# Two expert streams emitted in turn, row tile by row tile, with side work as jobs that hold a PSUM bank

## The chip, the core and the metric

The kernel runs on one core of a Trainium2 chip. The core has five engines that run their own instruction streams in order: TensorE (PE; its weight loads are shown apart as PEld), VectorE (DVE), ScalarE (ACT), GpSimd (POOL) and SyncE (SP, which issues most transfers). They wait for each other by semaphores. Data lies in SBUF; matmuls write to PSUM, which has eight banks of 128 partitions x 512 fp32 numbers. The metric is the device time of one execution in microseconds (us), lower is better. Times are medians of several executions, and one execution is recorded by the profiler.

## The reference

The program is two transformer blocks over 512 tokens of width 1024, all in fp32: a first block with a retention and pooling mixer, a mixture of experts and a gated projection, and a second block of attention. The change lies in the mixture of experts and in the step behind it:

```python
logits = xt @ router_w + router_b
top_vals, top_idx = lax.top_k(logits, 4)          # 4 of 32 experts for each token
gates = softmax(top_vals)
order = argsort(top_idx.reshape(-1)); tok = order // 4; xs = xt[tok]
gu = lax.ragged_dot(xs, w_gu, group_sizes) + b_gu[sorted_e]     # 1024 -> 2048
gate = minimum(gu[:, ::2], 7.0); up = clip(gu[:, 1::2], -7.0, 7.0)
act = (up + 1.0) * (gate * sigmoid(1.702 * gate))
y = lax.ragged_dot(act, w_down, group_sizes) + b_down[sorted_e] # 1024 -> 1024
out = zeros_like(xt).at[tok].add(y * gates[order][:, None])
...
h = h + out
gate = sigmoid(rms_norm(h, norm_ple_w) @ ple_gate_w); h = h + gate * (p @ ple_proj_w)
```

Each expert has 1024 x 2048 and 1024 x 1024 fp32 weights, 12 MB, which are read once.

## The kernel before

A fp32 product is made of three (or four) products of a shorter format: each operand is cut into a high part (a rounding copy) and a low part (the number minus its high part). For weights this is done on the chip. A row tile is 128 rows x 1024 columns of a weight matrix; ScalarE makes its high part `wh` (L877) and VectorE its low part `wl` (L878). An expert has 24 row tiles in three runs of 8: gate_up half 0, gate_up half 1, down. The function `chunks` (L864) walks over a run.

The experts are sorted by their count of tokens at run time, and the program alternates between a place for many and a place for few tokens (`LESS[e]`). A *few* expert has up to 64 tokens: high and low part of its x lie side by side as 128 columns, and a row tile takes 4 matmuls of 512 columns (L882). The two halves of the result are then added by the *fold*: ScalarE copies the accumulator to SBUF (`gs`, L939), and 8 matmuls with a constant put it, transposed and added, into a transposition bank (`tr`, L938). A *many* expert has up to 96 tokens: 6 matmuls of 512 columns a row tile (`mm3`, L165 to L167). The activation follows each gate_up run: two clamps on VectorE (`ag`, L910, and `au`, L911), read from the fold's bank or, for many, straight from the accumulator; a gelu on ScalarE (L912); a product on VectorE (L913); for many four transposes; then the split of the result `a` into its high part (ScalarE, L216) and low part (VectorE, L217). The same pair of lines splits the turned input `x`. After a down run the accumulator is scaled on ScalarE (`ys`, L948), and GpSimd adds its rows to the DRAM buffer `y_d` by an indirect transfer (L950). Rows of x come by an indirect gather (`xg`, L837), from tables (`slots`, L718 and on) that are made for batches of 2, 2, 4, 8, 8 and 8 experts.

The order of the work: expert e's runs come as gate_up half 0 of e, down of e-1, gate_up half 1 of e. As few and many experts alternate, so do their runs, by 8 row tiles. Side work (turning x, clamps, fold, scatter, tables) is a list of steps each due a fixed number of row tiles after it was put there (`later`, `next_tile`, L811 on). A scheduler in the framework then orders the instructions of each engine, so the program's order and the written one differ in places.

Buffers: weights arrive in 1 MB loads of two row tiles, issued by SyncE (`load`, L145) into seven buffers; the split pairs `wh`, `wl` are six. PSUM has three accumulators of two banks (`mm`) and two banks for transposes (`tr`). The gated bias of the down projection (`gated_bias`, L1026) is one product of the gates with the bias matrix; it uses four accumulators in turn (L1051) and is copied to `h` (L1052). The stage `back` loads `y_d` (L1154), adds it to `h` (L1159), multiplies by the norm's gain `g_ple` (L1160) and goes on to the next norm.

Of the kernel before, what the change touches and what calls it, by code (L numbers as in the profile page):

```python
# [18 lines left out]
S = 512  # L19
D = 1024  # L20
# [12 lines left out]
BATCHES = {0: 2, 2: 2, 4: 4, 8: 8, 16: 8, 24: 8}  # L33
# [16 lines left out]
def const_tables():  # L50
# [11 lines left out]
    t["sel"] = ((p[:, None] % 32 == np.arange(32)[None, :]) & (p[:, None] < 64)).astype(f32)  # L62
# [55 lines left out]
    return {"c_small": small, "c_lasting": lasting, "c_decay": decay, "c_band": band, "c_rope2": rope2}, cols  # L118


class Kern:
# [92 lines left out]
    def split_in(self, ps, dst, sl):  # L214
        dh, dl = dst
        self.nc.scalar.activation(dh[:, :, sl], ps, AF.Copy)  # L216
        self.nc.vector.tensor_tensor(out=dl[:, :, sl], in0=ps, in1=dh[:, :, sl].bitcast(F32), op=ALU.subtract)  # L217
# [91 lines left out]
    def run(self):  # L309
        tc, nc, I = self.tc, self.nc, self.I  # L310
        with ExitStack() as g:
# [8 lines left out]
            with ExitStack() as a:  # L320
# [382 lines left out]
    def slots_by(self, i0, n, T, ps, late=None):  # L703
# [23 lines left out]
        gi = T.tile([128, n], I32, tag=pre + "gi", name="gi")  # L727
        gt = T.tile([128, n], F32, tag=pre + "gt", name="gt")
# [8 lines left out]
    def arrange(self, P, T, sel):  # L737
# [14 lines left out]
        nc.vector.tensor_scalar(sel, c["ranks"][:, 0:NE], rank[:, 1:2], None, op0=ALU.is_equal)  # L752
# [30 lines left out]
    def moe(self, f, Q):  # L783
        tc, nc, I, c = self.tc, self.nc, self.I, self.c
        self.psum(f, "m", 3, 2)
# [3 lines left out]
        sel = P.tile([128, NE], F32R, name="sel")  # L789
# [3 lines left out]
        bt = P.tile([128, 2 * D], F32R, name="bt")  # L793
        nc.gpsimd.memset(bt.bitcast(F32)[64:128, :], 0.0)
        ys = P.tile([128, 2, D], F32, name="ys")
        braw = ys.rearrange("p a n -> p (a n)")
        for r in (0, 32):
            nc.scalar.dma_start(braw[r:r + 32, :], I["expert_b_gate_up"][0])
# [9 lines left out]
        self.at_tile, self.late = 0, []  # L808

        def later(stages):  # L810

            self.late += [(self.at_tile + d, fn) for d, fn in stages]

        def now(stages):
            for _, fn in stages:
                fn()

        def next_tile(n=1):
            self.at_tile += n
            while due := [a for a in self.late if a[0] <= self.at_tile]:  # L820
                a = min(due, key=lambda a: a[0])
                self.late.remove(a)
                a[1]()
# [5 lines left out]
        def table(e):  # L829

            ps = self.mm.tile([128, 2, 512], F32, tag="mm", name="mm")
            gen = self.slots_by(e, BATCHES[e], Q, ps[:, 0, :])
            later([(j, lambda: next(gen)) for j in range(BATCHES[e])] + [(BATCHES[e] + 2, lambda: tables(e, next(gen)))])

        def gather(e):
            m = FEW if LESS[e] else CAP
            nc.gpsimd.indirect_dma_start(out=xgs[e % 2][0:m], out_offset=None, in_=self.hn_d[:, :],  # L837
# [3 lines left out]
        def pair(m, tag):  # L841

            t = T.tile([128, 8, 2 * m], F32R, tag=tag, name=tag)
            return t[:, :, 0:m], t[:, :, m:2 * m], t

        def turned(x, m):

            p = pair(m, "x2")
            tp = {}

            def begin(j):
                tp[j] = self.transpose4(x, 4 * j, m=m)

            def end(j):
                self.split_in(tp[j], [a[:, 4 * j:4 * j + 4] for a in p[0:2]], slice(0, m))
            return p, [(1, lambda: begin(0)), (3, lambda: begin(1)), (4, lambda: end(0)), (6, lambda: end(1))]

        def turn(e):
# [714 lines left out]
```

## Time and profile before

| quantity | value |
|---|---|
| median of 3 runs | 1866.92 us (1865.54 to 1868.93) |
| profiled execution | 1864.25 us |
| its span | 1862.5 us, mean granted clock 0.979 |
| TensorE busy | 1762.6 us, 95% |
| VectorE busy | 1535.5 us, 82% |
| ScalarE busy | 1186.7 us, 64% |
| GpSimd busy | 188.2 us, 10% |
| DMA | 491.10 MB, mean 264 GB/s |
| first and last row tile of an expert | about 236.5 and 1392.6 us |

The experts take 1156 us of the 1862.5, from the first `wl` of L878 to the last. The rest lies before (the mixer) and after (the gated projection and the second block) and is left as it is, but for the first steps behind the experts. A share of busy time here is an average over stages with unlike limits, so the rows further down are cut from stretches inside the experts. A stretch of 48 row tiles is one many and one few expert. Matmuls are pipelined, so the spans of neighbouring matmuls overlap: the time from start to start is what one costs.

### The profile page before, as it was taken

The page shows a single profiled execution, that of the slowest core. Times are in us where ns is not written, and L with a number is a line of the kernel's source. Part 1 is how long each engine was busy: PE and PEld are TensorE (multiplying, and loading weights), DVE is VectorE, ACT ScalarE, POOL GpSimd, SP SyncE. Part 2 cuts the span into 40 slices and gives each one's busy share as a digit, 9 for nine tenths or more (in the row PEclk, how much of TensorE's full clock was granted, in tenths as well). Part 3 has the DMA queues.
Part 4 walks back from the last instruction along what each step waited for, and adds up shares of the span by engine and source line. Part 5 has one row for each costly group of instructions (what it writes and reads, how often), then busy time and mean ns, then how long its engine had stood idle before and what let it go on. Part 6 is the DMA issues. An engine that isn't in the chain of part 4 may idle for free.

```text
span 1862.5 us, 24800 instructions
## 1 busy us (share of the span) xinstructions
PE 1762.6 (95%) x8378; PEld 1278.2 (69%) x8379; DVE 1535.5 (82%) x2637; ACT 1186.7 (64%) x1584; POOL 188.2 (10%) x120
## 2 busy tenths in 40 slices
PE   8999779899999899999999999999998999999999
PEld 6887547666666566666666666666666877787776
DVE  5574479799999789999999999999987869999542
ACT  5224258677778777777877777877875545564431
POOL 0011210121111011311110210210100000000000
PEclk9999879999999899999999999999998999999999
DMA  8225568999999999999999999999986222211211
GB/s 282 89 85 170 164 208 314 335 367 373 361 381 375 337 340 380 336 387 386 370 388 389 344 381 386 372 383 389 361 310 217 91 66 64 91 46 46 85 57 40
DMA packets 147625, 491.10 MB, mean 264 GB/s; under 512 B 14273, under 2 KB 18625, under 8 KB 147424
## 3 DMA queue, kind: packets, MB, share of 16 engines
q1 hardware_dynamic: 137600, 462.02, 66.5%
q0 software_dynamic: 8064, 22.68, 5.3%
q10 hardware_dynamic: 1824, 4.72, 0.7%
q8 instruction: 68, 1.11, 0.2%
q14 instruction: 69, 0.57, 0.1%
HBM read 470.90 MB, written 23.07 MB: 265 GB/s over the span
## 4 chain that ended last, share of the span: by engine, by line
PE 37%; DVE 18%; ACT 4%; issue 4%; DMA 1%; SPq 0%; ACTq 0%; DVEq 0%
DVE wl L878 9%; PE mm L167 8%; PE mm L166 8%; PE mm L165 8%; PE mm L882 5%; ACT wh L877 3%; PE tr L938 2%; PE tr L205 2%; PE po L1389 2%; PE tr L1472 1%; DVE isc L1335 1%; PE tr L1445 1%; DVE wl L159 1%; DVE au L913 1%; DVE m L1334 1%
## 5 line engine op out<-in xcount | busy, mean ns | idle before, releaser
L878 DVE TENSOR_TENSOR wl<-wr,wh 128x1024 fp32r<-128x1024 f32 x762 | 889.3, 1217 | 31.8 <-ACT wh L877 31.0
L877 ACT ACTIVATE wh<-wr 128x1024 fp32r<-128x1024 f32 x762 | 747.0, 1049 | 23.9 <-PE mm L166 11.2
L167 PE MATMUL mm<-wl,x 128*96 128x512 f32 x512 | 207.7, 406 | 6.2 <-DVE wl L878 5.7
L882 PE MATMUL mm<-wl,x 128*128 128x512 f32 x512 | 180.8, 434 | 28.2 <-DVE wl L878 28.0
L165 PE MATMUL mm<-wh,x 128*96 128x512 f32 x512 | 204.8, 400 | 2.5 <-ACT wh L877 2.1
L166 PE MATMUL mm<-wh,x 128*96 128x512 f32 x512 | 203.6, 398 | 0.0
L882 PE MATMUL mm<-wh,x 128*128 128x512 f32 x512 | 166.8, 397 | 0.1
L882 PEld LDWEIGHTS mm<-wl,x 128*128 128x128 f32 x512 | 81.6, 189 | 98.9 <-DVE wl L878 91.1
L950 POOL DMA_INDIRECT y_d<-ys,gi x48 | 97.8, 2037 | 438.0 <-ACT ys L948 260.4
L167 PEld LDWEIGHTS mm<-wl,x 128*96 128x96 f32 x512 | 83.5, 163 | 53.9 <-DVE wl L878 22.1
L837 POOL DMA_INDIRECT xg<-hn_d,gi x32 | 59.0, 1844 | 591.2 <-PE tr L205 540.7
L165 PE MATMUL mm<-wh,x2h 128*128 128x512 f32 (+2 forms) x288 | 115.6, 401 | 3.2 <-ACT x2h L216 3.2
L882 PEld LDWEIGHTS mm<-wh,x 128*128 128x128 f32 x512 | 96.1, 189 | 26.0 <-ACT wh L877 0.7
L166 PE MATMUL mm<-wh,x2l 128*128 128x512 f32 (+2 forms) x288 | 112.5, 391 | 0.5 <-DVE x2l L217 0.5
L167 PE MATMUL mm<-wl,x2h 128*128 128x512 f32 (+2 forms) x288 | 112.0, 390 | 0.1
L159 DVE TENSOR_TENSOR wl<-wr,wh 128x2048 fp32r<-128x2048 f32 (+3 forms) x40 | 76.4, 1915 | 38.5 <-ACT wh L158 38.3
L166 PEld LDWEIGHTS mm<-wh,x 128*96 128x96 f32 x512 | 83.8, 164 | 34.2 <-DVE x L217 0.4
L165 PEld LDWEIGHTS mm<-wh,x 128*96 128x96 f32 x512 | 83.8, 164 | 33.4 <-ACT wh L877 3.0
L167 PE MATMUL mm<-wl,a 128*96 128x512 f32 x256 | 104.4, 408 | 1.9 <-DVE wl L878 1.8
L165 PE MATMUL mm<-wh,a 128*96 128x512 f32 x256 | 101.4, 396 | 0.0
L166 PE MATMUL mm<-wh,a 128*96 128x512 f32 x256 | 101.1, 395 | 0.0
L912 ACT ACTIVATE ag<-ag 96x512 f32<-96x512 f32 (+1 forms) x64 | 33.6, 525 | 100.9 <-DVE ag L910 100.8
(438 smaller groups left out, 3134.6 us busy)
## 6 DMA issues: line engine op xcount, KB each, us to landing
wr<-in_expert_w_gate_up_dram SPq DMA_DIRECT2D x253, 1024.0 KB, 8.4
wr<-in_expert_w_down_dram SPq DMA_DIRECT2D x128, 1024.0 KB, 9.3
wr<-in_w_in_dram SPq DMA_DIRECT2D x20, 1024.0 KB, 5.0
wr<-in_w_out_dram SPq DMA_DIRECT2D x8, 1024.0 KB, 4.9
wr<-in_ple_gate_w_dram SPq DMA_DIRECT2D x4, 1024.0 KB, 9.0
wr<-in_w_in_dram SPq DMA_DIRECT2D x4, 512.0 KB, 6.9
xt<-in_x_dram POOLq DMA_DIRECT2D x8, 256.0 KB, 5.4
y_d<-h ACTq DMA_DIRECT2D x4, 512.0 KB, 3.0
```

Source lines behind the costliest of these rows:

```text
L159: nc.vector.tensor_tensor(out=lo[:, sl], in0=raw[:, sl], in1=hi[:, sl].bitcast(F32), op=ALU.subtract)
L165: mm(out, a[0], b[0], start=first, stop=False)
L166: mm(out, a[1], b[0], start=False, stop=False)
L167: mm(out, a[0], b[1], start=False, stop=last)
L205: self.nc.tensor.transpose(ps[:, j, :], src[0:m, (i0 + j) * 128:(i0 + j + 1) * 128], self.c["ident"][0:m, 0:m])
L837: nc.gpsimd.indirect_dma_start(out=xgs[e % 2][0:m], out_offset=None, in_=self.hn_d[:, :], in_offset=bass.IndirectOffsetOnAxis(ap=tabs[e][0 ...
L877: nc.scalar.activation(hi, w[:, kk], AF.Copy)
L878: nc.vector.tensor_tensor(out=lo, in0=w[:, kk], in1=hi.bitcast(F32), op=ALU.subtract)
L882: nc.tensor.matmul(ps[:, n, :], pair[2][:, k, :], part[:, n * 512:n * 512 + 512], start=k == 0 and part is hi, stop=k == 7 and part is lo)
L938: nc.tensor.matmul(tp[0][:, 4 * s + b, :], v[:, b * 128:b * 128 + 128, s], c["fold"], start=True, stop=True)
L950: nc.gpsimd.indirect_dma_start(out=self.y_d[:, :], out_offset=bass.IndirectOffsetOnAxis(ap=rows[0:m // n], axis=0), in_=y[o:o + m // n], i ...
L1389: nc.tensor.matmul(po[:, hd, :], pt[:, a * (i + 1) + k, :], v[:, k, vcol(hd)], start=(k == 0), stop=(k == i))
```

## The change

The experts become two streams, one of the 16 many experts and one of the 16 few, each a generator that yields after every row tile of a run. The many stream begins alone; after 24 row tiles (`ALONE`) one row tile of each is emitted in turn until both end. Within a stream the order of the runs is as before, with e-1 now the stream's previous expert.

Side work becomes generators too (`job`): each yields the number of row tiles after which it goes on. A job that needs a transposition bank takes one of two by `bank()`, waits while none is free, and gives it back after its last reader (`free`); `LAG` = 5 row tiles lie between writing and reading it. Before a run needs what a job makes, `finish` drives the job to its end. High and low parts of a split lie a row tile apart. The tables are made in batches of 4 and in a single bank; a gather is issued by its own job, 16 row tiles before its rows are turned.

To make room, the last two weight buffers are now parts of `h`, which is not used in this stage otherwise; 8 in place of 10 loads are issued early. So the gated bias can't be kept in `h`: it is made in single banks, one half at a time, copied to SBUF (`yb`) and added to `y_d` by four more indirect transfers of 128 rows (line 1150 of the new program). Behind the experts `y_d` is loaded straight into `h` by four loads, all issued ahead of the gain's row, and the four adds go. The gate_up bias is kept in half as many columns, with two selectors.

```diff
-BATCHES = {0: 2, 2: 2, 4: 4, 8: 8, 16: 8, 24: 8}
+BATCHES = {0: 2, 2: 2, **{i: 4 for i in range(4, NE, 4)}}
+ALONE, LAG = 24, 5
...
-                    more = [f.enter_context(tc.tile_pool(name=f"wr4{i}", bufs=1, reuse_waits="tile")) for i in range(2)]
-                    self.wr = [wr, wr2, wr, wr2, wr2] + more
+                    self.wr = [wr, wr2, wr, wr2, wr2] + [Part(self.h[:, 2 * i:2 * i + 2, :]) for i in range(2)]
...
-        self.psum(f, "m", 3, 2)
+        self.psum(f, "m", 3, 1)
+        two = [self.tr, f.enter_context(tc.tile_pool(name="trn", bufs=1, space=bass.MemoryType.PSUM))]
...
+        def next_tile():
+            self.at_tile += 1
+            while due := [j for j in self.jobs if j[0] <= self.at_tile]:
+                step_job(due[0])
...
+        def bank():
+
+            while not two:
+                yield 1
+            pool = two.pop(0)
+            ps = pool.tile([128, 512], F32, tag="tr", name="tr")
+            return ps, lambda: two.append(pool)
...
+        def turned(x, m, p):
+
+            for j in range(2):
+                ps, free = yield from bank()
+                ps = ps[:, 0:4 * m].rearrange("p (n m) -> p n m", n=4)
+                for i in range(4):
+                    nc.tensor.transpose(ps[:, i, :], x[0:m, (4 * j + i) * 128:(4 * j + i + 1) * 128], c["ident"][0:m, 0:m])
+                yield LAG
+                for which in "hl":
+                    self.split_in(ps, [a[:, 4 * j:4 * j + 4] for a in p[0:2]], slice(0, m), which)
+                    yield 1
+                free()
+
+        def fetch(e, wait):
+
+            while e not in tabs:
+                yield 1
+            gather(e)
+            yield wait
+            m = FEW if LESS[e] else CAP
+            X[e] = pair(m, "x")
+            yield from turned(xgs[LESS[e]], m, X[e])
...
-            return [(3, lambda: nc.scalar.activation(gs, ps, AF.Copy)), (4, fold), (6, lambda: clamp(tp[0][:, 0:4], tp[0][:, 4:8])),
-                    (7, gelu), (8, mul),
-                    (9, lambda: self.split_in(up, [a[:, 4 * half:4 * half + 4] for a in p[0:2]], slice(0, FEW)))]
+            clamp(tp[:, 0:4], tp[:, 4:8])
+            free()
+            yield 1
+            gelu()
+            yield 1
+            mul()
+            yield 1
+            for which in "hl":
+                self.split_in(up, [a[:, 4 * half:4 * half + 4] for a in p[0:2]], slice(0, FEW), which)
+                yield 1
...
+            J[e, half] = job((folded if few else clamped)(ps, half, A[e]), LAG)
...
+                y = T.tile([128, D], F32, tag="yb", name="yb", bufs=1)
                 for n in range(2):
-                    nc.tensor.matmul(ps[:, n, :], gT[:, self.tok(t)], bs[:, n * 512:n * 512 + 512], start=True, stop=True)
-                later([(3, lambda: nc.scalar.activation(self.h[:, t, :], ps.rearrange("p a n -> p (a n)"), AF.Copy))])
-            later([(3, parts)] + [(4 + 8 * t, lambda t=t: products(t)) for t in range(NT)])
+                    ps, free = yield from bank()
+                    nc.tensor.matmul(ps, gT, bs[:, n * 512:n * 512 + 512], start=True, stop=True)
+                    yield LAG
+                    nc.scalar.activation(y[:, n * 512:n * 512 + 512], ps, AF.Copy)
+                    free()
+                nc.gpsimd.indirect_dma_start(out=self.y_d[:, :], out_offset=bass.IndirectOffsetOnAxis(ap=rows[:, t:t + 1], axis=0),
+                                             in_=y, in_offset=None, bounds_check=S - 1, oob_is_err=False, compute_op=ALU.add)
+                yield 8
...
+        def stream(es):
+
+            for e, after in zip(es, es[1:] + [None]):
+                at = es.index(e)
+                if after is not None:
+                    J[after, "x"] = job(fetch(after, 16))
+                if not LESS[e] and 4 * (at // 2) + 4 in BATCHES and at % 2 == 0:
+                    job(table(4 * (at // 2) + 4))
+                if e == 11:
+                    job(gated_bias())
+                yield from gate_up(e, 0)
+                if at and after is not None:
+                    yield from down(es[at - 1])
+                yield from gate_up(e, 1)
+            for e in es[-2:]:
+                yield from down(e)
...
+        many, few = (stream([i for i in range(ne) if LESS[i] == k]) for k in (False, True))
+        for _ in many:
+            next_tile()
+            if self.at_tile >= ALONE and next(few, 0) != 0:
+                next_tile()
...
         def routed(t):
+            nc.sync.dma_start(h[:, t, :], self.y_d[self.tok(t), :])
...
-            nc.vector.tensor_tensor(out=ht, in0=ht, in1=y, op=ALU.add)
```

Where the rows of the program stand, by engine. In the names, `mm` is an accumulator, `tr` a transposition bank, `wh` and `wl` the split pairs, `wr` and `h` weight buffers, `x` and `a` the turned inputs of gate_up and down.

TensorE before, in a many run (`x_10076` is a many expert's x) that follows a few run; `gs` is the copy of that few run's accumulator:

```order
L165 MATMUL mm<-wh_1903,x_10076 96x512
L166 MATMUL mm<-wh_1903,x_10076 96x512
L167 MATMUL mm<-wl_1904,x_10076 96x512
L165 MATMUL mm<-wh_1903,x_10076 96x512
L166 MATMUL mm<-wh_1903,x_10076 96x512
L167 MATMUL mm<-wl_1904,x_10076 96x512
L165 MATMUL mm<-wh,x_10076 96x512
L166 MATMUL mm<-wh,x_10076 96x512
L938 MATMUL tr<-c_small,gs 128x64 x4
L167 MATMUL mm<-wl,x_10076 96x512
L165 MATMUL mm<-wh,x_10076 96x512
L166 MATMUL mm<-wh,x_10076 96x512
```

The many run goes on alone for its 8 row tiles of 6 matmuls. The first row here begins its second row tile, and the first four matmuls of the few run's fold stand in its third one.

TensorE after, where both streams change from a gate_up run (`x`) to a down run (`a`):

```order
L188 MATMUL mm<-wh_1902,x 96x512
L189 MATMUL mm<-wl_1903,x 96x512
L187 MATMUL mm<-wh_1902,x 96x512
L188 MATMUL mm<-wh_1902,x 96x512
L189 MATMUL mm<-wl_1903,x 96x512
L942 MATMUL mm<-wh,a 128x512 x2
L1006 MATMUL tr<-c_small,gs 128x64 x4
L942 MATMUL mm<-wl,a 128x512 x2
L942 MATMUL mm<-wh,a 128x512 x2
L1006 MATMUL tr<-c_small,gs 128x64 x2
L942 MATMUL mm<-wl,a 128x512 x2
L1006 MATMUL tr<-c_small,gs 128x64 x2
```

Two row tiles of the many stream are followed by two of the few stream. The fold of the few run that has just ended stands among the first row tiles of the next few run, and both streams change their run at this place.

VectorE before, with a fold's clamp (`ag<-tr`) and a many clamp (`ag<-mm`):

```order
L878 TENSOR_TENSOR wl<-wr,wh 128x1024 x4
L910 TENSOR_SCALAR ag<-tr 128x256
L911 TENSOR_SCALAR au<-tr 128x256
L878 TENSOR_TENSOR wl_1902<-wr,wh_1901 128x1024
L913 SCALAR_TENSOR_TENSOR au<-au,ag 128x256
L878 TENSOR_TENSOR wl_1904<-wr,wh_1903 128x1024
L217 TENSOR_TENSOR a_11151<-au,a_11151 128x4x64
L878 TENSOR_TENSOR wl<-wr,wh 128x1024 x2
L910 TENSOR_SCALAR ag<-mm 96x512
L911 TENSOR_SCALAR au<-mm 96x512
L878 TENSOR_TENSOR wl<-wr,wh 128x1024 x2
```

Two row tiles are split between what a clamp needs and the clamp.

VectorE after, at a place where both clamps stand close together:

```order
L938 TENSOR_TENSOR wl<-h,wh 128x1024 x2
L938 TENSOR_TENSOR wl_1901<-h,wh_1900 128x1024
L938 TENSOR_TENSOR wl<-h,wh 128x1024
L938 TENSOR_TENSOR wl_1903<-wr,wh_1902 128x1024
L938 TENSOR_TENSOR wl<-wr,wh 128x1024
L970 TENSOR_SCALAR ag<-mm 96x512
L938 TENSOR_TENSOR wl<-wr,wh 128x1024
L938 TENSOR_TENSOR wl_1901<-wr,wh_1900 128x1024
L971 TENSOR_SCALAR au<-mm 96x512
L970 TENSOR_SCALAR ag<-tr 128x256
L938 TENSOR_TENSOR wl<-wr,wh 128x1024
```

The many clamp (`ag<-mm`) follows the split of the many run's last row tile directly here, and the fold's clamp comes two row tiles later.

## Rows read from the trace of the kernel before

**Rows 1.** Stretches: busy us (instructions) of PE, PEld, DVE, ACT, POOL; clock, DMA share, GB/s.

```profile
1187.20:1256.70 69.50, 68.02 (x305) 46.73 (x304) 64.31 (x69) 54.91 (x65) 8.75 (x5) 1.00 1.01 379
1256.70:1326.20 69.50, 68.02 (x305) 46.76 (x304) 64.25 (x69) 54.88 (x65) 7.43 (x4) 1.00 1.01 382
610.00:692.90 82.90, 74.31 (x317) 50.08 (x316) 67.81 (x73) 60.34 (x71) 8.15 (x5) 0.94 0.94 332
```

**Rows 2.** Waits, 1187.2 to 1256.7: engine line, waited for: us, times, longest.

```profile
PEld mm L882 <- DVE wl L878: 6.7, 16, 0.9
...
ACT x L216 <- PE tr L205: 2.4, 2, 1.8
DVE wl L878 <- ACT wh L877: 2.0, 4, 0.6
...
DVE ag L910 <- PE tr L938: 1.8, 2, 0.9
ACT gs L939 <- PE mm L882: 1.7, 2, 1.1
...
DVE a L217 <- ACT a L216: 1.1, 1, 1.1
...
DVE ag L910 <- PE mm L167: 0.3, 1, 0.3
```

**Rows 3.** Timeline of VectorE: start, us, what, count; eight `wl`.

```profile
1204.33 9.17 DVE L878 TENSOR_TENSOR wl<-wr,wh 128x1024 fp32r<-128x1024 f32 x8 [0.39 <-ACT wh L877]
```

**Rows 4.** Timeline of TensorE, three matmul rows and a fold half.

```profile
1214.11 0.40 PE L165 MATMUL mm<-wh,x 128*96 128x512 f32 x1
1214.34 0.39 PE L166 MATMUL mm<-wh,x 128*96 128x512 f32 x1
...
1215.27 1.04 PE L938 MATMUL tr<-c_small,gs 128*128 128x64 f32 x8
```

**Rows 5.** Waits of SyncE, 1187.2 to 1256.7.

```profile
SPq L145 <- DVE wl L878: 49.0, 22, 3.8
```

**Rows 6.** DMA, 1187.2 to 1256.7: rate in 40 slices, the sum, queues.

```profile
GB/s 420 422 413 413 417 427 403 405 403 321 276 325 217 285 380 424 422 415 408 427 417 408 413 424 382 363 398 403 349 349 264 278 323 363 413 420 417 314 389 431
DMA packets 6969, 26.31 MB, mean 379 GB/s; under 512 B 557, under 2 KB 557, under 8 KB 6965
...
q0 software_dynamic: 464, 1.18, 7.6%
```

**Rows 7.** Waits of VectorE, 300 to 1390.

```profile
DVE ag L910 <- PE tr L938: 31.3, 32, 4.0
DVE wl L878 <- ACT wh L877: 30.9, 59, 1.9
DVE a L217 <- ACT a L216: 14.4, 14, 1.1
...
DVE ag L910 <- PE mm L167: 5.2, 11, 2.7
```

**Rows 8.** Waits of the stretch with the gated bias, 610 to 692.9.

```profile
ACT h L1052 <- PE mm L1051: 7.1, 3, 5.7
...
ACT gs L939 <- PE mm L882: 4.8, 2, 4.3
```

**Rows 9.** DMA issues of 1187.2 to 1256.7: transfer, count, us to landing.

```profile
y_d<-ys,gi POOLq DMA_INDIRECT x3, 8.8
```

**Rows 10.** Timeline of GpSimd, the same stretch.

```profile
1246.52 2.12 POOL L950 DMA_INDIRECT y_d<-ys,gi  x1 [7.58 <-DMA y_d<-ys,gi]
```

**Rows 11.** Line 718: duration in ns, least, median, most; first and last start.

```profile
L718 DVE TENSOR_SCALAR oh<-b_iota,by_i x120: 234/243/523, 248.9 to 1034.7; 128x128 bf16<-128x128 bf16 x120
```

**Rows 12.** Timeline of VectorE behind the experts.

```profile
1413.57 1.23 DVE L1159 TENSOR_TENSOR h<-h,y 128x1024 f32<-128x1024 f32 x1 [2.47 <-DMA y<-y_d]
...
1416.34 1.23 DVE L1160 TENSOR_TENSOR y<-h,g_ple 128x1024 f32<-128x1024 f32 x1 [0.95 <-DMA g_ple<-in_norm_ple_w_dram]
```

**Rows 13.** Groups by line and shape, 1187.2 to 1256.7: busy us, mean ns.

```profile
L877 ACT ACTIVATE wh<-wr 128x1024 fp32r<-128x1024 f32 x49 | 47.8, 1049 | 0.0
...
L939 ACT ACTIVATE gs<-mm 128x1024 f32<-128x1024 f32 x2 | 2.1, 1028 | 1.7 <-PE mm L882 1.7
...
L910 DVE TENSOR_SCALAR ag<-mm 96x512 f32<-96x512 f32 x2 | 1.4, 683 | 0.3 <-PE mm L167 0.3
```

More of the change, by code (lines that the diff above doesn't have):

```diff
@@ L806, in moe, with job, step_job, finish @@
         parts += [[P.tile([128, 1024], F32R, name=f"w{k}{i}") for k in "hl"] for i in range(2)]
[L808 to L823, printed above, removed]
+        self.at_tile, self.jobs = 0, []
+        def job(gen, wait=0):
+            j = [self.at_tile + wait, gen]
+            self.jobs.append(j)
+            return j
+        def step_job(j):
+            try:
+                j[0] += next(j[1])
+            except StopIteration:
+                self.jobs.remove(j)
+        def next_tile():
+            self.at_tile += 1
+            while due := [j for j in self.jobs if j[0] <= self.at_tile]:
+                step_job(due[0])
+        def finish(j):
+            while any(j is k for k in self.jobs):
+                step_job(j)
+                if not two and (other := [k for k in self.jobs if k is not j]):
+                    step_job(other[0])
+        def bank():
[4 more added lines that the diff above has]
+            return ps, lambda: two.append(pool)
+        def now(gen):
+            for _ in gen:
+                pass
         def tables(e, t3):
@@ L841, in pair @@
         def pair(m, tag):
-            t = T.tile([128, 8, 2 * m], F32R, tag=tag, name=tag)
+            t = T.tile([128, 8, 2 * m], F32R, tag=f"{tag}{m}", name=tag)
             return t[:, :, 0:m], t[:, :, m:2 * m], t
[L846 to L858, printed above, removed]
-            X[e], stages = turned(xgs[e % 2], FEW if LESS[e] else CAP)
-            return stages
+        def turned(x, m, p):
[17 more added lines that the diff above has]
+            yield from turned(xgs[LESS[e]], m, X[e])
         A = {}
@@ L919, in clamped @@
             clamp, gelu, mul = glu(gt, up)
-            tp = []
-            return [(3, lambda: clamp(gu[:, :, 0], gu[:, :, 1])), (5, gelu), (6, mul),
-                    (7, lambda: tp.append(self.transpose4(up, m=CAP))),
-                    (10, lambda: self.split_in(tp[0], [a[:, 4 * half:4 * half + 4] for a in p[0:2]], slice(0, CAP)))]
+            clamp(gu[:, :, 0], gu[:, :, 1])
+            yield 2
+            gelu()
+            yield 1
+            mul()
+            tp, free = yield from bank()
@@ L929, in folded @@
+            yield 1
             v = gs.rearrange("p a (m s) -> p (a m) s", s=2)
+            tp, free = yield from bank()
+            tp = tp.rearrange("p (n m) -> p n m", n=8)
+            for s in range(2):
+                for b in range(4):
+                    nc.tensor.matmul(tp[:, 4 * s + b, :], v[:, b * 128:b * 128 + 128, s], c["fold"], start=True, stop=True)
+            yield LAG
             gt, up = (T.tile([128, 4, FEW], F32, tag=tag, name=tag) for tag in ("ag", "au"))
             clamp, gelu, mul = glu(gt, up)
-            tp = []
@@ L943, in scatter @@
+            free()
+            yield 1
+            gelu()
+            yield 1
+            mul()
+            yield 1
+            for which in "hl":
+                self.split_in(up, [a[:, 4 * half:4 * half + 4] for a in p[0:2]], slice(0, FEW), which)
+                yield 1
         def scatter(ps, gate, rows, n=1):
@@ L1198, in embed @@
             gated(t)
-            gather(t + 2, routed(t + 2))
+            gather(t + 2)
             normed(t)
```

190 lines of the change are left out of this document (107 added, 83 removed).

## The prediction

> **What bounds the kernel now.** Read the expert stage first, by stretches of one many and one few expert: 48 row tiles, cut at the 48th `wl` each. Two neighbouring stretches take 69.50 us each [rows 1]; see in them that the granted clock is full (1.00 of 2.4 GHz), VectorE is busy 64.3, TensorE 68.0, ScalarE 54.9, and the DMA share stands at 1.01. Three columns near 100% do not name the bound, so read the waits of that stretch next [rows 2]. VectorE's idle 5.2 us are there by cause: 2.0 for `wh`, 1.8 for the fold, 1.1 for `a`, 0.3 for a many accumulator. TensorE waits more, and for VectorE's `wl` (6.7 us, 16 times, with the next tile's columns in place). So the two hold each other up: TensorE starves in few runs, VectorE in front of what it reads from PSUM.
>
> Why they take turns is seen at the size of a run. A row tile costs VectorE 9.17/8 = 1.15 us [rows 3]. Matmuls of 512 columns start 0.23 us apart (1214.11, 1214.34) [rows 4], so a many tile costs TensorE 6 x 0.23 = 1.38, a few tile 4 x 0.23 = 0.92. A many run lets VectorE run ahead until the six split pairs are full; a few run lets TensorE catch up. Over a pair TensorE needs 248 x 0.23 = 57 plus two folds of 8 matmuls (about 1.0 each [rows 4]) per half and some transposes: about 62. VectorE needs 48 x 1.15 + 20 side operations of about 0.43 = 63.8, as its busy 64.3 says.
>
> The weights: SyncE waits 49.0 of 69.5 us for VectorE to give a buffer back [rows 5]; no row of the pair has an engine waiting for a weight transfer. The DMA view gives what the transfers could do: 413 to 431 GB/s in most slices, 217 to 363 where the indirect queue runs (it is 7.6% of the time) [rows 6]. Its slices above 360 without one average about 413; weighing the low ones in, I take 401 GB/s, my estimate: 26.31 MB / 401 = 65.7 us. That is the floor of a pair, 3.8 us under what it takes.
>
> Here the Trainium skill speaks against any gain: "DMA: Bandwidth & Descriptors", section "Where 436 GB/s comes from", says that for transfers between HBM and SBUF the HBM side, about 358 GB/s per core, binds, while the fabric could do 435. By 358 the pair could not take less than 73.5 us (an estimate); by 435 it could take 60.5. The trace disagrees with the first (379 and 382 GB/s in whole stretches) and lies near the second in slices without indirect traffic, as the page's own 425 for 16 MB on a lone core does.
>
> **The change part by part.** The work executed stays nearly the same; what moves is when. Terms are for the profiled execution, 1864.25 us (span 1862.5).
>
> *Fold.* Before, VectorE waits at the fold's clamp at each of the 32 half runs: 31.3 us, longest 4.0 [rows 7]. In the built order it now splits 4 row tiles beyond those that the fold stands behind in 17 of 32 places, 1 in 7. A tile's split is 1.15 us, so the lead pays for the fold's 1.0 us and the way to it: -31.3. *a.* The subtraction followed its copy at once and waited for it, 14.4 us in 14 places [rows 7]; the two now lie a row tile apart: -14.4. *wh.* The 30.9 us in 59 places [rows 7] have no part in the change: kept.
>
> *What is late next.* In 7 of 32 places the many clamp stands right behind the split of the last row tile of its own run, no tile ahead. VectorE is in order, so behind it wait the next `wl`s, and TensorE for those. Two row tiles of matmuls can stand before it at most: 12 x 0.23 = 2.8 us; the nearest row, this clamp's own wait of before, is 5.2 us over 11 places, longest 2.7 [rows 7], 0.5 a time. Between 0.5 and 2.8 I take 1.7, since the lead is smaller than before: 7 x 1.7 = +12. With no cover anywhere it would be 32 x 2.8 = 90; nothing supports that while 25 places keep two or more tiles.
>
> *Bias of the down projection.* The stretch that holds it takes 82.9 us [rows 1], 13.4 over a plain pair, with 3.5 of VectorE's work in it (67.8 against 64.3). The rest is order: a 5.7 us wait of ScalarE for the products, 4.3 for a few accumulator [rows 8], as the products take whole accumulators. In single banks and as jobs they do not: -8 of the 9.9. The four scatters that are new go to the POOL queue; one lands in about 8.8 us and the next waits 7.6 [rows 9, 10], so three in a row hold a gather back by some 27 us against its 16 tiles (23 us at 69.5/48): a slip of one gather costs 0 to 4, taken in the 1.9 left.
>
> *Tables.* 28 more small VectorE operations at 0.16 to 0.25 us (one-hot row 0.243) [rows 11] come to 4.5 to 7 us. Most were already paid in VectorE's gaps; of two thirds hidden, +3 is my middle (0 to 7). *First x of the second many expert.* It is turned right before its run: two waits for the transposes are 2.4 us in a pair [rows 2], once, +1.5 (0 to 5). *Head and tail.* 16 row tiles of many work that ran alone at 1.38 now lie beside few work, less the 24 tiles alone at the start: (1.38-1.15) x 16 = 3.7 gained at the end, up to 3 given back at the start: -1. *Behind the experts.* Four adds of 1.2 us go, but only the first lies on the path (1413.57); the product after it waited 0.95 us for the gain's row at 1416.34 [rows 12], which now is issued behind four loads instead of one. The two nearly cancel: -0.5 (-2 to +3).
>
> Sum: -31.3 - 14.4 + 12 - 8 + 3 + 1.5 - 1 - 0.5 = -38.7: 1864.25 - 38.7 = 1825.6. The median of before lies 2.7 above its profiled execution: 1828. Per pair that is about 67.3, over the 65.7 of the transfers and 63.8 of VectorE.
>
> **The rivals.** *Everything overlaps (D).* No new clamp wait and `wh` hidden too: a pair sinks to the floor of the transfers, 16 x 3.8 = 61, and 8 for the bias: 1867 - 69 = 1798. For it: TensorE 62 and VectorE 63.8 both fit. Against: the share of 1.01 leaves no slack, and `wh` waits are not touched.
>
> *Transfers are full already (B).* If 1.01 means that queues can give no more than 380 on average, indirect traffic included, every VectorE wait removed comes back as a wait for weights; 69.5 stays, and only bias and tables move, -5: 1862. For it: the share itself and slices as low as 217. Against: SyncE waits 49 us for buffers, and 420 to 431 is seen as soon as no indirect transfer runs.
>
> *The accumulators (C), slower.* In the built order both streams end and begin their runs at the same place, though they are said to run half a run apart: here the change doesn't do what it says. Three accumulators of two banks serve two open runs. So after a change the second stream's first matmul needs one of the two that just ended to be emptied: the few one by ScalarE's copy, 1.03 us [rows 13] behind up to two `wh` of 1.05, the many one by VectorE's two clamps of 0.68. What covers it is one many pair of tiles, 2.8 us, and a few pair, 1.8, if the third accumulator is free at that time: 4.6 against 3.1. If it is not, nothing covers, and TensorE with everything behind stands. There are about 45 such changes; at 1.2 us each, +54 and in sum +15: 1882. From 38.7/45 = 0.86 us per change it decides the sign. Before, runs ended one by one, 8 tiles apart, and ScalarE's wait for a few accumulator was 1.7 us a pair [rows 2]; that speaks for some price, hardly for all.
>
> **How the numbers follow.** Forecast 0.52, D 0.12, B 0.15, C 0.21. A measurement of this kernel can tell about 0.2% (3.7 us) from no change. Forecast, D and 0.04 of B are faster: 0.68; 0.10 of B is the same; C and 0.01 of B slower: 0.22. The forecast's own terms span 1810 to 1846 (new clamp waits 3.5 to 20, bias -10 to -2, `a` half kept 7). The range reaches past D to 1790, for `wh` waits that vanish in part, and to 1885 for C.
>
> **What would show it.** Right: the waits of VectorE for fold and `a` under 10 us together, a few places of 1 to 3 us before the many clamp, a steady pair of about 67 us, SyncE still waiting for VectorE, GB/s near 392. Wrong towards B: `wh` or `wl` waiting for weight transfers in most pairs. Wrong towards C: TensorE's first matmul of a run released by the copy or the clamp of an accumulator, about 45 times, over 0.86 us each.

## The result, and the profile after

The changed kernel takes 1834.14 us (median of 4 runs, 1830.95 to 1836.86) against 1866.45 of the kernel before beside it: a ratio of 0.9824, interval 0.9806 to 0.9843, or 32.3 us less. The forecast was 1828, its range 1790 to 1885. The profiled execution is the slowest of the four (1836.86 us, span 1835.0), so its rows explain 27.5 us of span.

Where they went: the first `wl` of an expert starts at 232.6 in place of 236.5 us (-3.9), the last one at 1361.5 in place of 1392.6, so the experts take 1128.9 in place of 1156.1 us (-27.2). From there to the end it is 473.5 in place of 469.9 (+3.6).

A pair below is a stretch of 48 row tiles, cut at every 48th `wl`; there are sixteen. The first view is the same as [rows 1], for a plain pair of the changed kernel, for the two longest of the four pairs in which the down bias is made or scattered, and for 300 to 1360 us as a whole:

```profile
1093.80:1162.10 68.30, 66.20 (x306) 47.26 (x305) 63.81 (x70) 55.47 (x65) 8.85 (x6) 1.00 1.02 384
...
664.80:743.50 78.70, 72.30 (x327) 51.11 (x326) 68.33 (x95) 58.06 (x70) 11.44 (x8) 0.93 1.02 363
812.50:886.80 74.30, 68.61 (x322) 47.28 (x321) 67.19 (x93) 56.26 (x65) 9.56 (x6) 1.00 1.02 373
```
```profile
300.00:1360.00 1060.00, 1018.66 (x4716) 722.73 (x4715) 990.75 (x1177) 846.95 (x983) 178.18 (x76) 1.00 1.02 379
```

A plain pair sinks from 69.50 to 68.3, not to the 67.3 of the forecast. From the third to the fifteenth the other pairs lie between 67.2 and 70.8, and these two at 78.7 and 74.3. The first, the second and the last take 81.6, 74.6 and 61.8 us, where they took 84.7, 76.0 and 66.3. The waits of VectorE from 300 to 1360, to be laid beside [rows 7]; one wait of before that is not shown there; and those of ScalarE, after and before:

```profile
DVE wl L938 <- ACT wh L937: 43.8, 59, 3.9
DVE ag L970 <- PE mm L189: 12.3, 7, 1.8
DVE ag L970 <- PE tr L1006: 4.4, 8, 0.6
DVE x L241 <- ACT x L239: 2.9, 3, 1.4
```
```profile
DVE gi L732 <- DMA y_d<-ys,gi: 6.8, 1, 6.8
```
```profile
ACT ys L1026 <- PE mm L942: 32.5, 15, 3.7
ACT gs L999 <- PE mm L942: 31.2, 25, 2.4
...
ACT wh L937 <- DMA wr<-in_expert_w_gate_up_dram: 19.0, 16, 2.1
...
ACT wh L937 <- DMA h<-in_expert_w_gate_up_dram: 7.3, 8, 1.9
...
ACT wh L937 <- DMA wr<-in_expert_w_down_dram: 4.8, 6, 2.1
ACT yb L1148 <- DMA y_d<-yb,rows: 4.3, 1, 4.3
ACT ys L1026 <- PE mm L189: 4.1, 5, 0.9
```
```profile
ACT gs L939 <- PE mm L882: 27.8, 30, 4.3
...
ACT ys L948 <- PE mm L882: 2.4, 2, 1.7
...
ACT ys L948 <- PE mm L167: 0.5, 1, 0.5
```

All waits of VectorE in this stretch fell from 90.2 to 67.8 us. The fold went from 31.3 to 4.4 us, `a` from 14.4 to nothing, a wait for a table's buffer (`gi`) of 6.8 us is gone, and the many clamp waits in 7 places, 12.3 us. What grew is the wait for `wh`, from 30.9 to 43.8 us. What stands behind it is found by going back, at each of its 59 places, along ScalarE's rows to the last wait that ScalarE itself had. In 40 places, 28.0 us, ScalarE had stood at `gs` or `ys` until TensorE ended a run; before the change that was 15.6 us. In 9 places, 7.6 us, it had waited for a weight, which it never did there before. 3.9 us stand behind `yb` and 4.4 behind transposes (11.1 before). One such place at the end of a few run's down, first ScalarE, then VectorE:

```profile
1150.23 1.12 ACT L1026 ACTIVATE ys<-mm,gt 128x1024 f32<-128x1024 f32 x1 [2.10 <-PE mm L942]
1151.25 2.00 ACT L937 ACTIVATE wh<-h 128x1024 fp32r<-128x1024 f32 x2
```
```profile
1152.33 2.36 DVE L938 TENSOR_TENSOR wl<-h,wh 128x1024 fp32r<-128x1024 f32 x2 [0.92 <-ACT wh L937]
```

The transfers are fuller too: a gate_up load of 1 MB takes 12.7 us to land, where it took 8.4 before, and the stage as a whole moves 379 GB/s where it moved 367:

```profile
DMA packets 106128, 401.38 MB, mean 379 GB/s; under 512 B 8029, under 2 KB 8029, under 8 KB 106053
```

### The profile page after: what moved, and what is told of

It reads as the page before. It is cut to its first block, busy times and chain, and to the rows that moved or that the text cites. A ratio compares the mean times of both kernels' runs of the same rounds, so it can differ in the third digit from the quotient of the medians.

```text
span 1835.0 us, 24671 instructions
## 1 busy us (share of the span) xinstructions
PE 1739.8 (95%) x8375; PEld 1285.0 (70%) x8379; DVE 1529.2 (83%) x2665; ACT 1193.9 (65%) x1591; POOL 221.2 (12%) x124
## 5 line engine op out<-in xcount | busy, mean ns | idle before, releaser
L938 DVE TENSOR_TENSOR wl<-wr,wh 128x1024 fp32r<-128x1024 f32 x550 | 641.8, 1215 | 30.9 <-ACT wh L937 30.1
L937 ACT ACTIVATE wh<-wr 128x1024 fp32r<-128x1024 f32 x550 | 544.1, 1050 | 46.3 <-DMA wr<-in_expert_w_gate_up_dram 19.0
L938 DVE TENSOR_TENSOR wl<-h,wh 128x1024 fp32r<-128x1024 f32 x216 | 252.9, 1215 | 13.8 <-ACT wh L937 13.8
L937 ACT ACTIVATE wh<-h 128x1024 fp32r<-128x1024 f32 x216 | 214.9, 1050 | 14.6 <-DMA h<-in_expert_w_gate_up_dram 7.3
L187 PE MATMUL mm<-wh,x 128*96 128x512 f32 x512 | 206.0, 402 | 0.7 <-ACT x L239 0.4
L1028 POOL DMA_INDIRECT y_d<-ys,gi x48 | 116.9, 2435 | 640.5 <-ACT ys L1026 390.8
L942 PE MATMUL mm<-wl,x 128*128 128x512 f32 x512 | 169.8, 412 | 1.4 <-DVE wl L938 1.2
L187 PE MATMUL mm<-wh,x2h 128*128 128x512 f32 (+2 forms) x288 | 114.6, 398 | 0.3 <-ACT x2h L239 0.3
L942 PEld LDWEIGHTS mm<-wl,x 128*128 128x128 f32 x512 | 89.0, 189 | 29.7 <-DVE wl L938 13.2
L187 PEld LDWEIGHTS mm<-wh,x 128*96 128x96 f32 x512 | 83.2, 163 | 31.3 <-ACT wh L937 3.5
L890 POOL DMA_INDIRECT xg<-hn_d,gi x32 | 67.6, 2114 | 291.4 <-PE tr L905 229.5
L187 PE MATMUL mm<-wh,a 128*96 128x512 f32 x256 | 102.2, 399 | 0.0
```

Source lines behind the costliest of these rows:

```text
L187: mm(out, a[0], b[0], start=first, stop=False)
L890: nc.gpsimd.indirect_dma_start(out=xgs[LESS[e]][0:m], out_offset=None, in_=self.hn_d[:, :], in_offset=bass.IndirectOffsetOnAxis(ap=tabs[e] ...
L937: nc.scalar.activation(hi, w[:, kk], AF.Copy)
L938: nc.vector.tensor_tensor(out=lo, in0=w[:, kk], in1=hi.bitcast(F32), op=ALU.subtract)
L942: nc.tensor.matmul(ps[:, n, :], pair[2][:, k, :], part[:, n * 512:n * 512 + 512], start=k == 0 and part is hi, stop=k == 7 and part is lo)
L1028: nc.gpsimd.indirect_dma_start(out=self.y_d[:, :], out_offset=bass.IndirectOffsetOnAxis(ap=rows[0:m // n], axis=0), in_=y[o:o + m // n], i ...
```

## The experiments

Times are medians; a ratio is to the kernel before, run in turn on the same chip, in brackets its 95% interval.

**Turns of 8 row tiles.**

```diff
-        for _ in many:
+        for i, _ in enumerate(many):
             next_tile()
-            if self.at_tile >= ALONE and next(few, 0) != 0:
-                next_tile()
+            if self.at_tile >= ALONE and i % 8 == 7:
+                for _ in range(8):
+                    if next(few, 0) != 0:
+                        next_tile()
```

> Undoes the turn by single row tiles alone: the two streams still run as generators, with jobs, single banks and a lag of 5 row tiles, but in turn by whole runs of 8. Lead theory (the gain comes from the row tiles that lie between what TensorE writes and VectorE reads, which jobs and lag keep): within 6 us of 1834, VectorE's waits for the fold and for a together under 12 us, against 45.7 before. Rival, balance theory (the gain comes from mixing tiles of 1.38 and 0.92 us, so that TensorE and VectorE need about the same in every stretch of two tiles): back to 1855 to 1870, TensorE starving in few runs again (more than 5 us a pair behind wl).

1897.53 us, ratio 1.0164 [1.0144, 1.0183]: slower than before. The waits of VectorE, then of TensorE, from 300 to 1400:

```profile
DVE wl L938 <- ACT wh L937: 60.2, 62, 15.5
DVE ag L970 <- PE tr L1006: 39.2, 27, 3.1
```
```profile
PE mm L942 <- DVE wl L938: 44.6, 93, 1.1
```

The fold waits 39.2 us again, and TensorE waits for `wl` in few runs, 44.6 us. The source keeps its lag of 5, but the scheduler did not: counted in the trace, the clamp stands only two row tiles behind the fold in 27 of 32 places, as in the kernel before (30 of 32). So this run does not part lead from turn. The places inside the runs do. In the table, the lead is the number of row tiles that VectorE splits beyond the one behind which the fold stands on TensorE; the last column is how many split row tiles TensorE had still to multiply when VectorE came to the clamp:

| run | row tiles in a turn | lead under 4: places, wait | lead 4 and more: places, wait | TensorE behind, mean |
|---|---|---|---|---|
| before | 8 | 32, 31.3 us | none | 2.1 |
| turns of 8 | 8 | 29, 39.2 us | 3, 0 us | 2.1 |
| turns of 4 (below) | 4 | 10, 4.0 us | 22, 0 us | 1.1 |
| changed kernel | 2 | 12, 4.5 us | 20, 0 us | 0.8 |
| lag of 2 (below) | 2 | 20, 4.9 us | 12, 0 us | 0.8 |
| emitted order (below) | 2 | none | 32, 0 us | 2.3 |

A clamp with a lead of four or more never waits, even where TensorE is 2.3 tiles behind. With a shorter lead it waits 1.0 and 1.4 us a place in turns of 8, 0.4 in turns of 4, and 0.2 to 0.4 in turns of 2. Both theories hold a part: a lead of four takes the wait away, and a short turn takes most of it.

This run is also some 31 us slower than the kernel before, which has the same turn and almost the same leads, and outside both expectations. The wait for `wh` is 60.2 us against 30.9, and 15.5 of that is one stall behind `yb`; what the rest of the change costs at this turn no run takes apart.

**Lag of 2** (`ALONE, LAG = 24, 2`).

> Undoes the lag alone: 2 row tiles in place of 5 between writing and reading a bank or an accumulator, with the streams in turn tile by tile. Lead theory: VectorE's waits for the fold, a and the many clamp come back, 25 to 45 us together in place of 17, and the time goes to 1850 to 1870. Balance theory: within 6 us of 1834.

1851.52 us, 0.9919 [0.9902, 0.9937]: the time that the lead theory asked for, but not by its waits.

```profile
DVE ag L970 <- PE mm L189: 8.7, 6, 1.8
DVE ag L970 <- PE tr L1006: 4.5, 8, 0.7
```
```profile
ACT yb L1148 <- DMA y_d<-yb,rows: 23.0, 2, 22.3
```

Fold and clamp wait no more than with a lag of 5, though the built order now has the short lead in 20 places in place of 12: the short turn covers them. One stall of 22.3 us is the difference: ScalarE stands at `yb`, the single buffer of the down bias, until its scatter has landed. That pair takes 94.0 us in place of 78.7, and the other fifteen together take 1050 us in both kernels. The lag matters here only through the bias, whose scatters then come in closer succession.

**Turns of 4** (as the first edit, with 4 for 8).

> The changed kernel with turns of 4 row tiles. Balance theory (what VectorE may be ahead and TensorE behind in a turn sets the waits, so time grows with the length of a turn from 2 row tiles at 1834 to 8 at 1897): 1842 to 1875. Rival (only turns longer than the six split pairs cost anything): within 6 us of 1834.

1858.85 us, 0.9960 [0.9946, 0.9974]. The many clamp waits 18.3 us in 14 places, the fold 3.7; a stall at `yb` of 20.3 us falls into this run too. The pair with the stall and the next take 161.3 us where the changed kernel has 147.4, the other fourteen 988.8 in place of 981.5. So turns of 4 cost some 7 us beside the stall. Turns of 8 cost some 54: without the pair of their own stall they take 1104 us in place of 1050. The cost grows with the turn, as the balance theory has it, and most of it comes between 4 and 8; that it begins at the six split pairs, as the rival has it, no run shows.

**Half the bytes.**

```diff
-                w = raw.pop(0) if raw else self.load(src(c0 * 128, 256).rearrange(...), 2, 1024)
+                w = raw.pop(0) if raw else self.load(src(c0 * 128, 128).rearrange(...), 1, 1024)
...
-                    nc.scalar.activation(hi, w[:, kk], AF.Copy)
-                    nc.vector.tensor_tensor(out=lo, in0=w[:, kk], in1=hi.bitcast(F32), op=ALU.subtract)
+                    kw = kk if raws else 0
+                    nc.scalar.activation(hi, w[:, kw], AF.Copy)
+                    nc.vector.tensor_tensor(out=lo, in0=w[:, kw], in1=hi.bitcast(F32), op=ALU.subtract)
```

Each load brings one row tile, which is split and multiplied twice: every instruction stays, half of the expert weights are left out.

> Leaves out half of the expert weights' bytes: after the early loads each load brings one row tile, which is used twice (other numbers, the same instructions on all engines). Transfers theory (in the changed kernel the DMA share of 1.02 binds in part, as the 31 us in which ScalarE waits for weights say): these waits go and the time falls by 12 to 30, to 1804 to 1822. Rival (VectorE and TensorE bind, transfers are hidden): less than 6 us, 1828 to 1834.

1785.19 us, 0.9569 [0.9554, 0.9584]: 49 less than the changed kernel, more than the transfers theory asked. But the scheduler had taken the smaller loads into account and put everything in another order (turns of 4 and 6 matmuls in place of 8 and 12), so order and bytes were mixed in this run. The same edit on the kernel before:

> The kernel before with half of the expert weights' bytes left out in the same way. Theory of the prediction (before the change no engine waits for weights, so they cost nothing): within 8 us of 1865. Rival (transfers bound it already, its DMA share of 1.01 says so): 1820 to 1850.

1803.97 us, 0.9667 [0.9652, 0.9681]. Outside both ranges. Here too the order had moved (the many clamp has a lead of three in all 32 places, where 27 had two), so the 62 us don't belong to the bytes alone. Whether any of them do is open: in the trace of the kernel before, ScalarE waits for no weight of an expert.

**Order and bytes apart.** A helper pins each row tile's instructions on its engine behind those of the tile emitted before (an edge of order without a wait):

```diff
+        def behind(engine, ins):
+            if engine in before:
+                tc.add_manual_dep(ins.ins, before[engine], mybir.DependencyInfo(
+                    mybir.DependencyClass.NoSync, mybir.DependencyReason.DATA), reason="in turn")
+            before[engine] = ins.ins.name
```

> The changed kernel with all its bytes, but on ScalarE, VectorE and TensorE each row tile is held behind the one emitted before it, so that the streams alternate by one row tile (4 and 6 matmuls) where the scheduler had made pairs (8 and 12). The run with half the bytes had this finer order too. Transfers theory (the 49 us that the half loads won came from the bytes): 1825 to 1837. Order theory (they came from the finer turn): 1785 to 1805.

1870.50 us, 1.0021 [1.0005, 1.0037]. Turns of one row tile are no gain: ScalarE's waits for weights rise to 78.6 us in its three largest rows (45.3, 20.0, 13.3). Neither theory had this.

> Half of the expert weights' bytes left out again (each load brings one row tile, which is used twice), but each row tile is held behind the one before and the streams take turns by two, 8 and 12 matmuls as in the changed kernel. Transfers theory: 1780 to 1795, as with half the bytes before. Order theory: 1822 to 1836, little won by the bytes alone.

1789.69 us, 0.9605 [0.9585, 0.9625], in the range of the transfers theory. But the helper holds only the row tiles; the side work had moved, and every fold has a lead of five or more. Now that very order with all bytes. The program is first built with the half loads, its order on the three engines is taken, and the second build is pinned to it:

```diff
+        for order in PLACED.values():
+            for i, j in zip(order, order[1:]):
+                tc.add_manual_dep(mine[j], mine[i].name, ...)
```

> All bytes, with the rows of TensorE, VectorE and ScalarE in exactly the order that the run with half the bytes and turns of two had (1790 us). In that order the scheduler, which took the loads for cheap, put the clamps further behind what they read. If bytes cost what they did at the emitted order (24.7 us between 1859.7 and 1835.0), 1808 to 1820, faster than the changed kernel by the order alone. If the bytes were the whole of the difference between 1834 and 1790, 1828 to 1840. If the order was the whole of it, 1786 to 1796.

1844.33 us, 0.9895 [0.9876, 0.9914]: the rows of the two runs stand in the same order on all three engines, so the bytes alone cost 54.6 us at this order, more than any of the three expected. The order that looked better is 10 us slower than the changed kernel's. It loses them in the first pair (90.8 us in place of 81.6) and in the last (65.4 for 61.8); the fourteen between take 982.3 in place of 985.5. The waits of VectorE and of ScalarE in it:

```profile
DVE a L246 <- ACT a L244: 32.2, 16, 14.8
DVE au L987 <- ACT ag L986: 26.2, 23, 2.5
DVE wl L952 <- ACT wh L951: 8.8, 13, 1.4
```
```profile
ACT wh L951 <- DMA wr<-in_expert_w_gate_up_dram: 51.4, 50, 2.6
ACT wh L951 <- DMA h<-in_expert_w_gate_up_dram: 19.8, 21, 2.9
ACT yb L1162 <- DMA y_d<-yb,rows: 13.8, 1, 13.8
...
ACT wh L951 <- DMA wr<-in_expert_w_down_dram: 8.2, 16, 2.9
```

No clamp waits at all and `wh` hardly; ScalarE waits 79.4 us for weights instead, and is late with `a` and `ag`: of all 69.2 us that VectorE waits here, 39.1 stand behind such a wait. With half the bytes no row of ScalarE's waits named an expert's weight. And it moves just what the changed kernel does:

```profile
DMA packets 107386, 405.38 MB, mean 379 GB/s; under 512 B 8067, under 2 KB 8067, under 8 KB 107307
```

**Emitted order.** All three engines pinned to the order of emission, in turns of two.

```diff
+        for ins in list(traced)[start:]:
+            if ins.engine in (mybir.EngineType.PE, mybir.EngineType.DVE, mybir.EngineType.Activation):
+                if ins.engine in before:
+                    tc.add_manual_dep(ins, before[ins.engine], ...)
+                before[ins.engine] = ins.name
```

> The changed kernel in turns of two row tiles, and in the expert stage everything on TensorE, VectorE and ScalarE, side work too, is held in the order in which it is emitted (the framework's scheduler may not move it). All bytes. Order theory (the side work's place in the built order makes the waits that half the bytes seemed to lift; the half loads had let the scheduler place it later): 1785 to 1810. Transfers theory (the bytes bind): 1822 to 1845.

> The same with half of the expert weights' bytes left out (each load brings one row tile, used twice); the rows of TensorE, VectorE and ScalarE are the same as in the run with all bytes. Transfers theory: 30 to 55 us under it. Order theory: within 8 us of it.

1859.66 us, 0.9966 [0.9952, 0.9979], outside both ranges, and 1834.97, 0.9840 [0.9825, 0.9855]: 24.7 us for the bytes, less than the transfers theory's 30 to 55 and far more than the order theory's 8. By pairs, 13.7 of these us lie in the three from 687.7 to 906.7 us, in which the bias's scatters run (73.0, 76.0 and 70.0 against 66.9, 71.6 and 66.8). The waits of TensorE with all bytes show the rival of the accumulators at work (L1051 and L187 are first matmuls of runs):

```profile
PE mm L1051 <- ACT ys L1026: 24.1, 12, 2.9
PE mm L187 <- ACT gs L999: 10.9, 9, 2.9
PE mm L1051 <- ACT gs L999: 7.4, 7, 2.7
```

42.4 us in 28 places, 1.5 each. ScalarE, in turn, stands at no `gs` or `ys` here. Yet a plain pair (1251.4 to 1316.4) runs at 65.0 us with all bytes, a busy TensorE and 395 GB/s, and the same pair with half the bytes at 64.8. The pairs from the second to the fifteenth take 978.3 us where the changed kernel has 985.5. What this order loses, it loses above all in the first pair, 104.9 us in place of 81.6, in which ScalarE waits 26.0 us for the first columns of the early `wh` that VectorE writes (2.1 in the changed kernel):

```profile
ACT wh L937 <- DVE wh L936: 26.0, 13, 4.1
```
```profile
233.20:338.10 104.90, 83.24 (x336) 52.06 (x337) 77.25 (x127) 60.61 (x69) 11.48 (x5) 0.84 0.69 230
...
1251.40:1316.40 65.00, 65.00 (x305) 48.42 (x304) 64.24 (x70) 55.09 (x65) 11.53 (x3) 1.00 1.02 395
```

**The step behind the experts.**

```diff
-            nc.sync.dma_start(h[:, t, :], self.y_d[self.tok(t), :])
+            y = T4.tile([128, D], F32, tag="t4", name="y")
+            nc.sync.dma_start(y, self.y_d[self.tok(t), :])
+            return y
...
+            nc.vector.tensor_copy(ht, y)
```

> Undoes the step behind the experts alone: y_d is loaded into a buffer of its own, one load ahead of the gain's row and the others later, and VectorE copies it to h at the price of the add of before (1.2 us, four times). Order theory (the change put ScalarE's sum of squares of h, which waits 10.3 us for its load, ahead of the copies of TensorE's products, so TensorE stands 5.9 us and its clock falls): 3 to 5 us faster, 1829 to 1831. Rival (the copies cost what the adds did and nothing is won): 1834 to 1838.

1835.11 us, 0.9831 [0.9814, 0.9848] against 0.9824: no difference, the rival's time. The trace shows the part of the theory that holds. The first product with the gain starts at 1385.91, where the changed kernel has it at 1393.04, with a last `wl` that is 0.9 us later; first the old step, then the changed kernel:

```profile
1385.91 1.23 DVE L1272 TENSOR_TENSOR y<-h,g_ple 128x1024 f32<-128x1024 f32 x1 [1.36 <-DMA g_ple<-in_norm_ple_w_dram]
```
```profile
1393.04 1.21 DVE L1270 TENSOR_TENSOR y<-h,g_ple 128x1024 f32<-128x1024 f32 x1
```

From the last `wl` to the end this profile has 470.5 us in place of 473.5. By the medians nothing is left of it, and the runs scatter by more (1828.69 to 1836.44), so the price of this step stays open.

**Both repairs on the emitted order** (the old step, and the four bias parts 24 row tiles apart in place of 8).

> All in emitted order, turns of two, and two repairs: the four parts of the down bias 24 in place of 8 row tiles apart (its buffer is free by then, ScalarE does not wait 4.3 us for its scatter and the clock does not fall), and the old step behind the experts. Against the run without the repairs 4 to 12 us faster, if the stall of the bias is what its 10 us in the changed kernel's pair of 78.7 were; not faster, if these us were its work.

1856.87 us, 0.9954 [0.9940, 0.9967], against 0.9966 without: 2.8 us, under the 4 that were expected at least, and the intervals overlap. The pairs with the bias fell from 73.0 and 76.0 to 69.8 and 73.7 us. No version ran faster than the changed kernel with all its bytes. Here too it is the first pair that decides: the fourteen in the middle take 973.2 us where the changed kernel has 985.5. An emitted order with a mended start was not tried.

## Why the prediction was right, and where it was not

The sign and the time hold: 6 us above the point, within the forecast's own range of 1810 to 1846. The mechanism holds in part: VectorE's waits for fold and `a` went, and that is most of the gain. That the point came so close is also luck, since terms were missed in both directions. Of its signs, the waits for fold and `a` under 10 us and the few places before the many clamp came; the steady pair stands at 68.3 us and 384 GB/s, not at 67 and 392; and the sign for B came in part, with waits for weights in 10 of 16 pairs. By its steps:

- *Fold and `a`*, -45.7: the rows give 31.3 + 14.4 before and 4.4 after, -41.3. The step counted the row tiles that VectorE may run ahead in the built order, and where there are four or more (20 places) nothing waits. The 7 places with a lead of one, which it had counted and given no price, hold 4.1 of the 4.4 us. What it left out is the turn. In the 5 places with a lead of two the clamp waits 0.4 us in all, where it waited 0.85 in each of 30 such places before: TensorE is 0.8 row tiles behind at a clamp, and no longer 2.1.
- *The many clamp*, +12 in 7 places at 1.7: 12.3 us in 7 places, 1.76 each. The places were read from the built order. The price was the middle between 0.5 and 2.8, and that it was hit so well is luck. The sum should have taken off the 5.2 us of before, so the term was 7.1.
- *`wh`*, kept at 30.9: 43.8. This is the step that failed: the prediction took the wait to have no part in the change. In its place the runs show that ScalarE stands 67.8 us in front of `gs` and `ys` until TensorE ends a run (30.7 before), and 28.0 us of the wait for `wh` come behind that, against 15.6. Another 7.6 us come behind ScalarE's new waits for weights, which the prediction had put at nothing down to a floor of 65.7 us a pair. 22.1 of ScalarE's 33.9 us for weights lie in three pairs that each hold a batch of tables: the transfers bind in stretches. No run mended either cause in this order, so what each is worth in time is not shown.
- *Tables* +3, *first x* +1.5, *head and tail* -1: the first and the last pair together went from 151.0 to 143.4 us, -7.6, far more than head and tail were given. A batch of tables for four experts costs a pair 1.0 to 2.5 us, where one for eight cost 3.4 to 4.6, so in all the tables cost about the same; and the wait of 6.8 us for `gi` went, which the prediction did not have. The first x is not seen by itself.
- *Bias*, -8: 13.4 us over a plain pair before. After, the four pairs with it lie 17.4 over four plain ones; two table batches at 1.0 to 2.5 us in them are not its own, so 12 to 15 are left. Nothing was won that the rows can tell. The product's wait for accumulators went, as forecast; in its place ScalarE waits 4.3 us for the single `yb` and the next `wl` 3.9 behind it. TensorE stands 2.9 us behind that, and from 691.2 to 701.5 its granted clock is 1.2 in place of 2.4 GHz, which makes the 0.93 of this pair; the pair of before had 0.94 [rows 1]:

```profile
690.23 0.60 ACT L1148 ACTIVATE yb<-tr 128x512 f32<-128x512 f32 x1 [4.25 <-DMA y_d<-yb,rows]
```

  The prediction had looked at POOL's queue for these scatters, not at who waits for the buffer they read.
- *Behind the experts*, -0.5: from the last `wl` to the end +3.6 by the profile. ScalarE's sum of squares reads `h` and waits 10.3 us for its load, with a copy of TensorE's products queued behind it, where before the copy came first (VectorE's side of that is in [rows 12]):

```profile
1383.77 1.06 ACT L251 ACTIVATE junk<-h 128x1024 bf16<-128x1024 f32 x1 [10.32 <-DMA h<-y_d]
1384.73 0.19 ACT L251 ACTIVATION_READ_ACCUMULATOR junk<-h 128x1 f32 x1
1384.83 0.58 ACT L1646 ACTIVATE pp<-mm 128x512 f32<-128x512 f32 x1
```

  The step counted VectorE's adds and the gain's row and left ScalarE's queue out; by time it could not be told from nothing.
- *Start*: no term, -3.9; no run says why.

The rivals. D (the floor): not reached, 68.3 a pair. B (transfers full): its forecast of no gain was wrong; its mechanism took back a part, 7.6 us of VectorE's waits in the trace. The 24.7 and 54.6 us that the bytes cost hold for two other orders. The Trainium skill, "DMA: Bandwidth & Descriptors", section "Where 436 GB/s comes from", puts the bound of the HBM side at about 358 GB/s for a core, as half of what two cores share. The trace does not agree: the whole stage moved 379. This program runs on one core, and the prediction had left that condition out. C (accumulators): both streams do change runs together, and in the changed kernel TensorE waits for no copy of an accumulator. ScalarE stands ready in front of `gs` and `ys` instead, and the price comes as the wait for `wh`. Held in emitted order it is the other way round: ScalarE never stands there, and TensorE waits 1.5 us in each of 28 places, where the rival had 1.2 in 45. That wait is not time lost one for one: the pairs between the first and the last are no slower for it (978.3 against 985.5 us).

## What to carry to other kernels

When two engines hold each other up through a small set of buffers, two things take the wait away: more work between a write and its reader, and turns short enough that the writer is never far behind. Count the first in the built order and not in the source: a lag of 5 became a lead of 2 in one run. Before keeping a wait as it is, ask what the engine in front of it will have to stand for after the change: waits removed here came back as ScalarE's, for the end of a run and for weights. And when an experiment makes a transfer smaller, see that the order of the program is the same, else two things are measured as one.

## What the runs showed of the hardware

Over the expert stage the changed kernel and the order copied from the half loads both moved 379 GB/s, with the indirect queue beside it, while single slices of 1.7 us show up to 431 [rows 6]; the best pair kept up 395. From 300 to 1360 us of the changed kernel, slices of 1.7 us in which the indirect queue has a tenth of the DMA time or more moved 322 GB/s on average, slices with none of it 397. Not every low slice is one of these: the tenth and eleventh of [rows 6], 321 and 276 GB/s, have none of the indirect queue, though the prediction's floor had read all low slices so. Halving the bytes did not shorten the work on them: `wl` takes 1215 ns and `wh` 1052 with half the bytes, 1216 and 1050 with all. What the bytes cost with the order held shows as waits, 39.1 of the 69.2 us of VectorE's in the copied order.
